# Weight sums in place, two blocks per split, first rows on VectorE, and a mixed order of pairs in a transformer-block kernel

## The chip, the core and the metric

The kernel runs on one core of a Trainium2 chip. The metric is the device time of one execution in microseconds (us); lower is better. In the rows the engines are PE (TensorE, matmuls; PEld its weight loads), DVE (VectorE), ACT (ScalarE), POOL (GpSimd) and SP (SyncE, which here issues DMAs only).

## The reference

One layer over 1024 positions of width 1024, all in float32:

- u = rmsnorm(x); z = u @ w_in gives a_b, a_c, a_x (512 each), q_lat (384), kv_lat (256), k_rope (32), gate_a, gate_b (1024 each)
- a gated causal width-3 depthwise convolution of these, and latent attention (8 heads, low-rank keys and values, rotary part, block-causal mask); h = x + rmsnorm((sigmoid(gate_a) * ya + sigmoid(gate_b) * yb) @ w_o)
- up = conv3(rmsnorm(h) @ w_ffn_up) + b, width 2 x 2816; f = (gelu(up_gate) * up_val) @ w_ffn_down; h = h + rmsnorm(f)
- out = h + rmsnorm((p @ w_ple_proj) * sigmoid(h @ w_ple_gate))

## The kernel before, in words

Everything is kept transposed: 128 features on the partitions, 1024 positions along the row, cut into two halves of 512. On-chip memory is dealt by hand as 51 numbered slots of 1024 float32 per partition (`f32(i)`, `single(i, h)` for a half); eight groups of four adjacent slots (`QUADS`) can be read by one instruction over four halves.

A float32 operand is used as two rounded parts: `split` makes `hi` by a ScalarE cast (L174) and `lo = src - hi` by a subtraction on VectorE or GpSimd (L175). A product of 128 x 512 outputs then takes three passes (hi hi, lo hi, hi lo). `block` splits one 512-wide half of a weight tile into one slot of the ring `wblk` (hi in the slot's first half, lo in its second); the ring has seven slots.

The three large matrix products (w_in, w_ffn_up, the first 16 of 22 row blocks of w_ffn_down) are done by a Winograd form of Strassen's scheme, seven block products for eight. The right operand's seven combinations (B11, B21, B22, T2, T4, T3, T1) come from `x_blocks` in three stages, all on VectorE but for the casts: `first` (B11, B21), `second` (B22, T2 and four 128x2048 subtractions, L268), `third` (T3, T4, T1). `second` needs the second half of the positions, `first` only the first half. The left side comes as pairs of weight tiles: `pair` loads two tiles, forms S1 to S4 (L325 to L327, L363), and runs seven products of 12 matmuls each (`prod`, L289). `first_row` runs two of the seven ahead (A11 B11 and A12 B21), while the right operand's other combinations are still being made; the pair that follows runs the other five (`early`). S1 stands in a half slot of its own (ring `s1s`), and the T1 product is copied out by ScalarE (L358) into another (`m5s`) and added by GpSimd (L359).

Stages: the norm of x and the p projection (to about 43 us), six first rows and the pairs of the gates, convolution mixer and latents (to 370), projections and attention (to 630), w_o and a norm, twelve first rows of the up projection (to 830), its 22 pairs (to 1200: first the twelve with a first row, of which eight had been stored to DRAM in `d_z` and are loaded again, then ten without), down in two groups of four first rows and four pairs and a plain tail (to 1437), then the second norm and the last gate. After each up pair the two results go through the convolution (ScalarE L517, four VectorE steps L519, in PSUM), the gelu (L897) and a product (L898), and the tile goes to DRAM (`d_f`); down loads these tiles again into four-slot groups (`u0`, `u1` in `plans`), and the lists in `plans` say which slots hold which combination. In down's second group the results are added to the first group's (`add`).

A scheduler writes each engine's instruction order: it takes what is ready by its own estimate of times, earlier program text first. On the chip each engine keeps that order; a waiting instruction holds all behind it.

Of the kernel before, what the change touches and what calls it, by code (L numbers as in the profile page):

```python
# [57 lines left out]
class Ring:  # L58
# [6 lines left out]
    def __call__(self):  # L65
        self.n += 1
        return self.items[(self.n - 1) % len(self.items)]


@with_exitstack  # L70
def kernel(
# [170 lines left out]

    who = dict(S1=G, S3=G, bS1=V, bS3=G, bS4=G, fw=G)

    def x_blocks(u, slots):

        names = ("B11", "B21", "B22", "T2", "T4", "T3", "T1")
        where = {n: slots[4 * i : 4 * i + 4] for i, n in enumerate(names)}
        B = {}
# [16 lines left out]
        def sub(dst, a, b):  # L266
            d, a_, b_ = (several(u[k : k + 4], F32, h) for k, h in (dst, a, b))
            V.tensor_sub(d, a_, b_)  # L268

        def second():  # L270
# [6 lines left out]
            sub(b21, b21, b22)  # L277
# [243 lines left out]
    for g in range(2):  # L521
        ys = [34, 35]
        v, e = f32(47), f32(48)
        for j in range(2):
            ct = 2 * g + j
            pair(w_in[4 + ct], w_in[8 + ct], B, raws, s1s, m5s, mm, v, e)
# [4 lines left out]
        pair(w_in[2 * g], w_in[2 * g + 1], B, raws, s1s, m5s, mm, v, e)  # L531
# [24 lines left out]
    m5s = Ring(singles(50))  # L556
# [18 lines left out]
    raws = Ring([7, 8])  # L575
    lraw = Ring([46, 45, 47])
# [255 lines left out]
    u = list(range(34, 42))  # L832
# [283 lines left out]
```

## Time and profile before

| | |
|---|---|
| time, median of 3 runs | 1557.64 us (1552.98 to 1557.90) |
| profiled execution, its own time | 1554.84 us |
| its span, first to last instruction | 1553.0 us |
| mean granted TensorE clock | 0.986 of full |
| DMA moved | 195.59 MB, 126 GB/s |

Idle time of an engine matters only where TensorE waits for it.

### The profile page before, as it was taken

The numbers are of one execution on the slowest core, as the hardware profiler recorded it, in microseconds if no ns is written. First come the engines' busy times: TensorE is split into PE (matmuls) and PEld (weight loads), VectorE is DVE, ScalarE is ACT, GpSimd is POOL, SyncE is SP. The second block draws the span as 40 slices with busy tenths as digits, with TensorE's granted clock in tenths as the row PEclk, the third lists the DMA queues.
The fourth block names the chain that finished last, engine by engine and source line by source line (L and its number), as shares of the span: only waits on it lengthen the run. The fifth ranks groups of instructions, "written<-read, shape, count | busy, mean of one in ns | idle before, by whom it ended". The sixth has DMA issues, their size and how long they took to land. (4 is left out here: it accounts for less than half of the span.)

```text
span 1553.0 us, 19627 instructions
## 1 busy us (share of the span) xinstructions
PE 1483.4 (96%) x6980; PEld 1228.1 (79%) x6980; DVE 1161.7 (75%) x1645; ACT 726.4 (47%) x1266; POOL 759.9 (49%) x561
## 2 busy tenths in 40 slices
PE   8999999999989999999998999999999897999997
PEld 6778888887768888888886876788887785788786
DVE  6996666656478887925688899888878879648776
ACT  8534323445357777334444544444445343234533
POOL 3744454427344334434355434444434465687853
PEclk9999999999999999999999999999999999999998
DMA  9334222326831013624362433322224533253322
GB/s 335 128 125 179 86 91 68 122 96 230 267 116 52 28 56 110 205 78 149 106 236 67 161 141 117 108 88 90 91 85 163 176 95 117 87 164 108 127 91 96
DMA packets 72642, 195.59 MB, mean 126 GB/s; under 512 B 7264, under 2 KB 22112, under 8 KB 72544
## 3 DMA queue, kind: packets, MB, share of 16 engines
q1 hardware_dynamic: 64192, 169.89, 33.0%
q10 hardware_dynamic: 8352, 24.44, 4.1%
q8 instruction: 55, 0.90, 0.2%
q14 instruction: 43, 0.35, 0.1%
HBM read 142.79 MB, written 51.51 MB: 125 GB/s over the span
## 5 line engine op out<-in xcount | busy, mean ns | idle before, releaser
L289 PE MATMUL psum<-s,s 128*128 128x512 f32 x3948 | 921.2, 394 | 33.0 <-DVE s L175 8.1
L289 PEld LDWEIGHTS psum<-s,s 128*128 128x128 f32 x3948 | 744.8, 190 | 203.7 <-DVE s L175 12.6
L175 POOL TENSOR_TENSOR s<-s,s 128x512 fp32r<-128x512 f32 (+1 forms) x298 | 441.2, 1492 | 379.2 <-ACT s L174 363.5
L174 ACT CAST s<-s 128x512 fp32r<-128x512 f32 (+2 forms) x572 | 357.8, 657 | 452.8 <-PE psum L289 128.4
L202 PE MATMUL psum<-s,s 128*128 128x512 f32 (+1 forms) x1920 | 412.4, 373 | 12.3 <-ACT s L174 10.5
L202 PEld LDWEIGHTS psum<-s,s 128*128 128x128 f32 x1920 | 335.7, 191 | 73.3 <-ACT s L174 13.3
L175 DVE TENSOR_TENSOR s<-s,s 128x512 fp32r<-128x512 f32 (+2 forms) x274 | 280.6, 1037 | 48.7 <-ACT s L174 45.5
L519 DVE SCALAR_TENSOR_TENSOR psum<-s,vecs,psum 128x1023 f32<-128x1023 f32 (+1 forms) x88 | 111.5, 1281 | 19.3 <-ACT psum L517 17.9
L237 DVE TENSOR_TENSOR s<-s,s 128x512 f32<-128x512 f32 (+1 forms) x83 | 74.9, 903 | 56.9 <-ACT s L234 54.6
L326 POOL TENSOR_TENSOR s<-s,s 128x512 f32<-128x512 f32 x47 | 68.5, 1458 | 96.3 <-DMA s<-in_w_up_dram 42.9
L325 POOL TENSOR_TENSOR s<-s 128x512 f32<-128x512 f32 x47 | 65.0, 1384 | 93.8 <-DMA s<-in_w_up_dram 32.7
L359 POOL TENSOR_TENSOR s<-s,s 128x512 f32<-128x512 f32 x43 | 57.8, 1344 | 92.0 <-ACT s L358 91.8
L175 DVE TENSOR_TENSOR s<-psum,s 128x512 fp32r<-128x512 f32 (+3 forms) x144 | 70.9, 505 | 31.3 <-ACT s L174 30.2
L174 ACT CAST s<-psum 128x512 fp32r<-128x512 f32 (+3 forms) x144 | 61.1, 444 | 36.0 <-PE psum L774 9.8
L750 POOL TENSOR_SCALAR s<-s,ri 128x384 f32<-128x384 f32 (+5 forms) x48 | 41.3, 861 | 70.3 <-DVE ri L749 55.5
L363 DVE TENSOR_TENSOR s<-s 128x512 f32<-128x512 f32 x47 | 49.5, 1054 | 30.9 <-POOL s L175 30.6
L234 ACT ACTIVATE s<-s 128x512 f32<-128x512 f32 (+1 forms) x82 | 47.8, 590 | 52.8 <-DVE s L1004 23.9
L737 PE MATMUL psum<-s,s 128*128 128x512 f32 (+2 forms) x288 | 67.4, 359 | 2.3 <-ACT s L748 2.2
L327 DVE TENSOR_TENSOR s<-s,s 128x512 f32<-128x512 f32 x47 | 44.6, 948 | 22.4 <-POOL s L326 22.0
L517 ACT ACTIVATE psum<-s,vecs 128x1024 f32<-128x1024 f32 x44 | 52.8, 1207 | 17.4 <-POOL s L359 11.4
L762 PE MATMUL psum<-s,s 128*128 128x256 f32 x320 | 54.1, 292 | 1.5 <-DVE s L175 0.7
L748 ACT ACTIVATE s<-psum,nm 128x128 f32<-128x128 f32 (+3 forms) x64 | 47.5, 745 | 14.2 <-DVE nm L746 9.0
(116 smaller groups left out, 1122.9 us busy)
## 6 DMA issues: line engine op xcount, KB each, us to landing
s<-in_w_up_dram SPq DMA_DIRECT2D x56, 512.0 KB, 3.7
s<-in_w_in_dram SPq DMA_DIRECT2D x40, 512.0 KB, 3.7
s<-in_w_down_dram SPq DMA_DIRECT2D x36, 512.0 KB, 3.6
d_f<-s SPq DMA_DIRECT2D x22, 512.0 KB, 2.7
s<-d_f SPq DMA_DIRECT2D x22, 512.0 KB, 5.4
s<-in_x_dram SPq DMA_DIRECT2D x32, 256.0 KB, 5.4
d_sg<-s ACTq DMA_DIRECT2D x16, 512.0 KB, 2.9
s<-d_sg SPq DMA_DIRECT2D x16, 512.0 KB, 3.9
```

Of the source, the lines that this page charges most:

```text
L174: A.copy(hi, src)
L175: (eng or V).tensor_sub(lo, src, f(hi))
L202: nc.tensor.matmul(out_ps, w[c // HALF][pw][:, c % HALF : c % HALF + P], X[k][half][px][:, cs], start=start and a == 0 and k == 0, stop=st ...
L237: V.tensor_add(acc, acc, sq)
L289: nc.tensor.matmul(pt, w[pw][:, k * P : (k + 1) * P], blk[k][px], start=a == 0 and k == 0, stop=a == 2 and k == 3,)
L325: who["S1"].tensor_add(s1, a21, a22)
L326: who["S3"].tensor_sub(a21, a11, a21)
L359: G.tensor_add(d22, d22, m5)
L517: A.activation(dst, src, AF.Identity, bias=bias, scale=w2)
L519: V.scalar_tensor_tensor(dst[:, i:], src[:, : S - i], w, dst[:, i:], op0=ALU.mult, op1=ALU.add)
L737: nc.tensor.matmul(st_[:, lo_ : lo_ + w_], q[part_q][:, o : o + P], parts(K[hd, kh])[part_k][:, 0:w_], start=part_q == 0 and part_k == 0, ...
L762: nc.tensor.matmul(po[:, 0:256], vt[:, kt, :], t_[:, kk * 256 : (kk + 1) * 256], start=kt == 0 and part == 0, stop=kt == 2 * b + 1 and par ...
```

## The change

- `pair`: S1 overwrites a22 (after a22 is split for the T4 product), S3 overwrites a21, S2 overwrites a11, and S4 overwrites a12. The rings `s1s` and `m5s` are gone. `wide` splits a whole weight tile at once: hi of both blocks in one slot, lo in another. A11/A12, S2/S4 and S3/S1 are split so; A22 alone by `block`. The order of products becomes A11, A12, S2, S3, S1, A22, S4. The T1 product is added twice by VectorE. `who` names the engines of A11/A12's split, A22's split and the two sums.
- `first_row`: the weights' split is one `wide` on VectorE.
- `x_blocks`: the order of stage three is T3, T1, T4, and its VectorE instructions are queued behind the last subtraction of stage two.
- The slots freed join `wblk`: nine slots in the gate and up stages.
- Up: the twelve pairs with a first row stand between the ten without (0 without, 1 with, 2 without, ...); the convolution of a pair comes after the next pair in the program; the last tile's comes inside down's first group.
- Down: another dealing of slots; each group's first pair has its splits and sums on VectorE; the plain tail's six tiles come by halves through one slot.

```diff
+    def become(self, items):
+
+        k = self.n % len(self.items)
+        old = self.items[k:] + self.items[:k]
+        self.items = [i for i in items if i not in old] + [i for i in old if i in items]
+        self.n = 0
...
+    def wide(src, eng):
+        hi, lo = f32r(wblk()), f32r(wblk())
+        split(src, hi, lo, eng)
+        return [(hi[:, hs(i)], lo[:, hs(i)]) for i in range(2)]
...
-        names = ("B11", "B21", "B22", "T2", "T4", "T3", "T1")
+        names = ("B11", "B21", "B22", "T2", "T3", "T1", "T4")
...
         def third():
-            operand("T3", 0, 1)
-            operand("T4", 4, 0)
-            operand("T1", 0, 0)
+            with tc.issue_after(t4[0].ins):
+                operand("T3", 0, 1)
+                operand("T1", 0, 0)
+                operand("T4", 4, 0)
...
-        w = load_w(src, raws, eng=who["fw"])
+        raw = f32(raws())
+        nc.sync.dma_start(raw, src)
+        w = wide(raw, V)
...
+    def pair(src0, src1, B, raws, banks, out0, out1, early=False, hooks=(), add=None, who=(V, G, G, G)):
...
         if not early:
-            A11 = block(a11, V)
-        s1 = single(*s1s())
-        who["S1"].tensor_add(s1, a21, a22)
-        who["S3"].tensor_sub(a21, a11, a21)
-        V.tensor_sub(a11, s1, a11)
-        S2 = block(a11, V)
-        S3 = block(a21, who["bS3"])
+            A11, A12 = wide(r0, who[0])
+        A22 = block(a22, who[1])
+        who[2].tensor_add(a22, a21, a22)
+        who[3].tensor_sub(a21, a11, a21)
+        V.tensor_sub(a11, a22, a11)
+        V.tensor_sub(a12, a12, a11)
+        S2, S4 = wide(r0, V)
+        S3, S1 = wide(r1, V)
+        m1, u3 = (d12, d21) if add is None else add
+        u2 = m1
         if not early:
             A.copy(m1, times(A11, "B11"))
+            V.tensor_add(d11, times(A12, "B21"), m1)
         V.tensor_add(u2, times(S2, "T2"), m1)
         V.tensor_add(u3, times(S3, "T3"), u2)
-        A22 = block(a22, V)
-        pt = times(A22, "T4")
...
+        pt = times(S1, "T1")
...
+        V.tensor_add(d22, u3 if add is None else d22, pt)
         V.tensor_add(d12, d12, pt)
...
-            m5 = single(*m5s())
-            A.copy(m5, pt)
-            G.tensor_add(d22, d22, m5)
-        if not early:
-            A12 = block(a12, G)
-            V.tensor_add(d11, d11, times(A12, "B21"))
-        V.tensor_sub(a12, a12, a11)
-        S4 = block(a12, who["bS4"])
+        V.tensor_add(d21, d21, times(A22, "T4"))
         pt = times(S4, "B22")
...
+    wblk.become([*range(NBLK), 33, 50])
...
+    wblk.become([*range(NBLK), 45, 50])
...
+    rows = [1, 3, 5, 7, 8, 10, 11, 13, 14, 16, 18, 20]
+    early = dict(zip(rows[:4], (44, 33, 46, 47)))
+    spilled = rows[4:]
...
+        pair(w_up[j], w_up[NFF + j], B, raws, mm, f32(z0), f32(z1), j in early or j in spilled, who=(G, G, G, G))
...
+    last = up(0)
+    for j in range(1, NFF):
+        now = up(j)
+        gated(*last)
+        last = now
...
     plans = (
-        (range(9, 13), range(21, 25), [29, 25, 38, 13, 0, 17, 21]),
-        (range(9, 13), range(29, 33), [13, 17, 0, 21, 38, 25, 29]),
+        (range(9, 13), range(13, 17), [21, 25, 29, 38, 17, 0, 9]),
+        (range(13, 17), range(21, 25), [25, 38, 17, 0, 9, 29, 13]),
     )
+    u3s = singles(24)
...
+        raws = Ring([7, 8] if g else [7, 8, 45])
...
         second()
+        if g == 0:
+            free = [50]
+            gated(*last)
         third()
...
+                add=(m1s[i], single(*u3s[i % 2])) if g else None, who=(V, G, G, G) if i else (V, V, V, V),
             )
+            mm = Ring(range(6))
...
+    fops = [[*range(25, 29), 38, 39], [*range(29, 33), 17, 18]]
+    fraw = Ring(singles(21))
```

## Rows read from the trace of the kernel before

**Rows 1.** Busy time of each engine over the span: us, share, instructions.

```profile
PE 1483.4 (96%) x6980; PEld 1228.1 (79%) x6980; DVE 1161.7 (75%) x1645; ACT 726.4 (47%) x1266; POOL 759.9 (49%) x561
```

**Rows 2.** Windows: stretch, length, busy us (instructions) of PE, PEld, DVE, ACT, POOL, PEclk, DMA.

```profile
43.00:100.00 57.00, 53.45 (x225) 43.38 (x224) 56.06 (x59) 27.33 (x40) 33.51 (x18) 0.94 0.29 95
100.00:370.00 270.00, 270.00 (x1216) 224.14 (x1215) 176.01 (x255) 110.31 (x186) 129.74 (x95) 1.00 0.36 124
800.00:842.00 42.00, 35.30 (x136) 26.09 (x135) 39.24 (x34) 17.78 (x24) 19.35 (x12) 0.92 0.22 67
...
875.00:1000.00 125.00, 119.12 (x509) 94.06 (x508) 117.21 (x124) 55.74 (x76) 55.02 (x41) 1.00 0.37 126
1000.00:1173.00 173.00, 173.00 (x765) 143.26 (x764) 133.76 (x161) 79.67 (x113) 69.83 (x54) 1.00 0.26 86
1173.00:1225.00 52.00, 46.31 (x190) 37.15 (x189) 50.16 (x42) 28.06 (x38) 24.09 (x14) 0.93 0.41 146
...
1275.00:1330.00 55.00, 45.71 (x180) 34.95 (x179) 50.23 (x42) 20.78 (x32) 33.18 (x21) 0.94 0.31 105
1330.00:1371.00 41.00, 39.11 (x170) 31.37 (x169) 27.34 (x32) 13.93 (x25) 31.91 (x23) 1.00 0.37 107
```

**Rows 3.** Windows inside two of the switches between matrix products.

```profile
801.00:834.00 33.00, 26.30 (x105) 18.89 (x103) 33.00 (x27) 15.31 (x22) 14.19 (x8) 0.97 0.17 48
...
1185.00:1213.00 28.00, 22.31 (x94) 17.60 (x93) 27.96 (x19) 15.49 (x20) 14.64 (x9) 0.96 0.37 130
```

**Rows 4.** Groups by line and form: shapes, count, busy us, mean ns, idle before.

```profile
L175 POOL TENSOR_TENSOR s<-s,s 128x512 fp32r<-128x512 f32 x290 | 433.3, 1505 | 360.7 <-ACT s L174 345.0 <-PE psum L202 10.3 <-PE psum L762 1.8
...
L175 DVE TENSOR_TENSOR s<-s,s 128x512 fp32r<-128x512 f32 x217 | 196.6, 911 | 41.3 <-ACT s L174 38.2 <-PE psum L289 1.3
L175 DVE TENSOR_TENSOR s<-s,s 128x1024 fp32r<-128x1024 f32 x52 | 79.8, 1566 | 4.2 <-ACT s L174 4.2
...
L325 POOL TENSOR_TENSOR s<-s 128x512 f32<-128x512 f32 x47 | 65.0, 1384 | 93.8 <-DMA s<-in_w_up_dram 32.7 <-DMA s<-in_w_down_dram 18.1 <-DVE s L175 13.5
...
L174 ACT CAST s<-s 128x1024 fp32r<-128x1024 f32 x52 | 52.8, 1049 | 47.5 <-DVE s L268 31.4 <-DVE s L175 9.4 <-DVE s L858 3.0
...
L338 DVE TENSOR_TENSOR s<-psum,s 128x512 f32<-128x512 f32 x47 | 32.2, 685 | 17.9 <-PE psum L289 9.8 <-issue 4.7 <-ACT s L337 3.4
...
L898 DVE TENSOR_TENSOR s<-s,psum 128x1024 f32<-128x1024 f32 x22 | 26.7, 1214 | 2.3 <-ACT s L897 2.3
...
L268 DVE TENSOR_TENSOR s<-s,s 128x2048 f32<-128x2048 f32 x8 | 20.9, 2616 | 0.0
```

**Rows 5.** DVE in order of time in one up pair: start us, us, instruction.

```profile
957.27 0.68 DVE L339 TENSOR_TENSOR s<-psum,s 128x512 f32<-128x512 f32 x1
957.87 1.27 DVE L519 SCALAR_TENSOR_TENSOR psum<-s,vecs,psum 128x1022 f32<-128x1022 f32 x1
959.05 1.23 DVE L175 TENSOR_TENSOR s<-s,s 128x512 fp32r<-128x512 f32 x1
...
964.86 1.77 DVE L327 TENSOR_TENSOR s<-s,s 128x512 f32<-128x512 f32 x1 [0.71 <-POOL s L326]
```

**Rows 6.** PE in order of time: runs of matmuls, idle before and releaser.

```profile
954.42 3.04 PE L289 MATMUL psum<-s,s 128*128 128x512 f32 x12 [0.82 <-DVE s L338]
...
970.18 1.19 PE L289 MATMUL psum<-s,s 128*128 128x512 f32 x4 [0.74 <-DVE s L338]
...
1211.76 28.62 PE L289 MATMUL psum<-s,s 128*128 128x512 f32 x113 [4.69 <-DVE s L306]
...
1292.24 15.83 PE L289 MATMUL psum<-s,s 128*128 128x512 f32 x60 [3.30 <-ACT s L358]
1310.59 4.17 PE L289 MATMUL psum<-s,s 128*128 128x512 f32 x16 [2.51 <-ACT s L174]
...
1320.16 20.82 PE L289 MATMUL psum<-s,s 128*128 128x512 f32 x84 [1.52 <-DVE s L175]
```

**Rows 7.** POOL in order of time at down's second group.

```profile
1307.71 2.17 POOL L325 TENSOR_TENSOR s<-s 128x512 f32<-128x512 f32 x1 [4.64 <-DVE s L175]
```

More of the change, by code (lines that the diff above doesn't have):

```diff
@@ L525 @@
             ct = 2 * g + j
-            pair(w_in[4 + ct], w_in[8 + ct], B, raws, s1s, m5s, mm, v, e)
+            pair(w_in[4 + ct], w_in[8 + ct], B, raws, mm, v, e)
             V.tensor_mul(v, v, e)
@@ L575 @@
     raws = Ring([7, 8])
+    wblk.become(range(NBLK))
     lraw = Ring([46, 45, 47])
@@ L829 @@
             split(ya_, *mX[ft][h])
-    u = list(range(34, 42))
+    u = [*range(38, 42), *range(34, 38)]
     wos = load_all(w_o, raws, range(25, 34))
@@ L862 @@
             second()
-    s1s = Ring(singles(50))
-    m5s = Ring([(45, 1)])
-    zs, ts_ = Ring([34, 35, 36, 37]), Ring([48, 49])
+    wblk.become([*range(NBLK), 45, 50])
+    free = [48, 49, 34, 35, 36, 37]
     tps = Ring([4, 6])
-    early = [44, 33, 46, 47]
-    spilled = 8
-    NE = len(early) + spilled
-    for j in range(NE):
-        z0 = f32(early[(j - NE) % len(early)])
+    rows = [1, 3, 5, 7, 8, 10, 11, 13, 14, 16, 18, 20]
+    early = dict(zip(rows[:4], (44, 33, 46, 47)))
+    spilled = rows[4:]
+    for n, j in enumerate([*spilled, *early]):
+        z0 = f32([*early.values()][n % 4])
         first_row(w_up[j], B, raws, mm, z0[:, hs(0)], z0[:, hs(1)])
-        if j < spilled:
+        if j in spilled:
             nc.sync.dma_start(d_z[j], z0)
@@ L880, with up, gated @@
     mm = Ring(range(4))
-    for n, j in enumerate([*range(spilled, NE), *range(spilled), *range(NE, NFF)]):
-        if n:
-            late = [z0, z1]
-        z0 = early[n] if n < len(early) else zs()
-        z1 = zs()
-        if n < len(early):
-            zs.items.append(z0)
-        if len(early) <= n < NE:
+    def up(j):
+        z0 = early[j] if j in early else free.pop(0)
+        if j in spilled:
             nc.sync.dma_start(f32(z0), d_z[j])
-        pair(w_up[j], w_up[NFF + j], B, raws, s1s, m5s, mm, f32(z0), f32(z1), n < NE)
+        z1 = free.pop(0)
+        pair(w_up[j], w_up[NFF + j], B, raws, mm, f32(z0), f32(z1), j in early or j in spilled, who=(G, G, G, G))
+        return j, z0, z1
+    def gated(j, z0, z1):
         cv = []
@@ L895 @@
             cv.append(t)
-        fo = f32(ts_())
-        A.activation(fo, cv[0], AF.Gelu_apprx_tanh)
-        V.tensor_mul(fo, fo, cv[1])
-        nc.sync.dma_start(d_f[j], fo)
-    mm = Ring(range(6))
-    raws = Ring([7, 8])
-    late = [z0, z1, *late]
-    rest = [i for i in zs.items if i not in late]
-    yacc = [i for two in zip(rest, late) for i in two]
-    extra = [42, 43, 48, 49]
+        fo = free.pop(0)
+        A.activation(f32(fo), cv[0], AF.Gelu_apprx_tanh)
+        V.tensor_mul(f32(fo), f32(fo), cv[1])
+        nc.sync.dma_start(d_f[j], f32(fo))
+        free.extend([z0, z1, fo])
+    last = up(0)
[3 more added lines that the diff above has]
+        last = now
+    raws = Ring([7, 8])
+    wblk.become(range(NBLK))
+    extra = [i for i in free if i not in quad_of][-2:]
+    free = [i for i in free if i not in extra]
+    yacc = [i for two in zip(free[:4], [*free[4:], *last[1:]]) for i in two]
+    extra = [42, 43, *extra]
+    m1s = [single(*i) for i in singles(45, 50)]
     plans = (
-        (range(9, 13), range(21, 25), [29, 25, 38, 13, 0, 17, 21]),
-        (range(9, 13), range(29, 33), [13, 17, 0, 21, 38, 25, 29]),
+        (range(9, 13), range(13, 17), [21, 25, 29, 38, 17, 0, 9]),
+        (range(13, 17), range(21, 25), [25, 38, 17, 0, 9, 29, 13]),
     )
+    u3s = singles(24)
     for g, (u0, u1, starts) in enumerate(plans):
@@ L956, in down @@
         V.tensor_add(y, y, pt)
-    fs = [(c, f_tiles(ks)) for c, ks in ((16, range(16, 20)), (20, range(20, 22)))]
-    hrs = Ring(singles(38, 39))
-    sqs, sqs2, accs = Ring(singles(48)), Ring(singles(49)), Ring(singles(50))
+    fs = ((16, fX[:4]), (20, fX[4:]))
+    hrs = Ring(singles(24, 21))
+    sqs, sqs2, accs = Ring(singles(extra[2])), Ring(singles(extra[3])), Ring(singles(50))
     hX = [[None, None] for _ in range(8)]
+    hslots = range(9, 17), [*range(17, 21), *range(38, 42)]
     SS, RB = 6, 7
@@ L985 @@
                 for o in range(c_ * n, (c_ + 1) * n):
-                    down(fX, w, h, o)
+                    down(fX_, w, h, o)
         second_residual(h)
```

81 lines of the change are left out of this document (25 added, 56 removed).

## The prediction

> **What bounds the kernel now.** I read the busy times first, then the windows, then each window's waits. The reader sees TensorE at 96% of the span and VectorE, next, at 75% [rows 1], so an edit counts only where TensorE starts late. The windows give its pace: from 1000 to 1173 us it starts 765 matmuls and never stops, 173.0/764 = 226.4 ns each; 100 to 370 is as dense [rows 2]. The change leaves the number of matmuls alone (2 products per first row, 5 per pair behind one, 7 per whole pair, 12 matmuls each), so it can give back only lost time: a window's length less its starts times 226.4 ns [rows 2]:
>
> - A, 43 to 100 (switch to the gates' pairs): 57.0 - 225 x 0.2264 = 6.1 us
> - B, 800 to 842 (switch to the up projection): 42.0 - 30.8 = 11.2
> - C, 875 to 1000 (up pairs behind a first row): 125.0 - 115.2 = 9.8
> - D, 1173 to 1225 (up to down): 52.0 - 43.0 = 9.0
> - E, 1275 to 1330 and 1330 to 1371 (down's first to second group): 14.2 + 2.5 = 16.7
>
> That is 52.8 us of the execution's 1554.84 (span 1553.0, 1.84 around it). At the switches VectorE has no gap: 33.00 of 33 us at B, 27.96 of 28 at D [rows 3]. TensorE's stops there end on it, directly (4.69 at 1211.76, 1.52 at 1320.16) or through ScalarE behind it (3.30 at 1292.24) [rows 6]. In C one pair takes 970.18 - 954.42 = 15.76 us [rows 6] where 60 matmuls take 13.6: VectorE's work for a pair is longer than TensorE's.
>
> **Prices.** VectorE reading PSUM: the next instruction 0.60 us later, a convolution step 1.18 later [rows 5]; 128x1024 from PSUM 1.21, near 1.13 as a step [rows 4]. With both sources in SBUF a 128x512 one is as short when GpSimd rests, but 1.77 beside it [rows 5]; over the run 0.91 at 512 wide, 1.57 at 1024, 2.62 at 2048 [rows 4]. PSUM-sourced ones stay at 0.68 [rows 4]. So GpSimd's work slows exactly the splits and sums. GpSimd takes 1.50 for a split, 1.38 for a sum [rows 4].
>
> **The change part by part.**
>
> *Pairs (47).* The weight sums go into the loaded tiles, two blocks are split by one 1024-wide cast and subtraction, and the copy of the T1 product with its GpSimd addition becomes a second VectorE addition from PSUM. On VectorE a pair behind a first row had 5 SBUF steps and 5 PSUM steps; it gets 2 sums, 2 wide splits and 6 PSUM steps: 2 x 0.60 + 2 x 1.13 + 6 x 0.60 = 7.1 clean against 6.0. On GpSimd it has one split and two sums, 4.25, for two splits and three sums, 7.1. Per pair VectorE works 1.1 more and waits less.
>
> *C, the mixing of the up projection.* With convolution (4 x 1.18) and product (1.13) a short pair costs VectorE 7.1 + 5.85 = 12.95 clean. Before it was 6.0 + 5.85 = 11.85 in a cycle of 15.76 that was almost all VectorE, so about 3 to 4 us were contention; GpSimd's share of it falls by 4.25/7.1, so I take 1.8: 14.75 (bounds 12.95, no contention, and 16.9, all of it). A whole pair adds one PSUM step, 13.55, and, as GpSimd there also splits A11 and A12 (a 128x1024 subtraction, not in this trace: between 1.50 and 2 x 1.50; I take 2.8, nearer the second, since the length doubles), about 2.5 contention: 16.0. TensorE has 13.6 and 19.0. Before, the twelve short ones ran in a row, each 2.2 late, and the slack of the ten whole ones came after; now at most two short ones stand together, 2.3 us behind, and the whole pair next to them has 3.0 to spare. In sum VectorE needs 12 x 14.75 + 10 x 16.0 = 337 of TensorE's 12 x 13.6 + 10 x 19.0 = 353. So C's 9.8 go to about 2: gain 7.5, bounds -6 (16.9 per short pair: 12 x 3.3 less 10 x 2.4) and 9.8.
>
> A rule weighed here: a VectorE instruction with two SBUF sources took 1.77 instead of 0.68 beside GpSimd [rows 5]. The Trainium skill (SBUF — State Buffer, section Who interferes with whom) calls it an exclusive lock held for a whole instruction, the later one blocked fully. It speaks against the wide GpSimd split: by it a VectorE sum could wait 2.8 where 1.5 was the most, 10 x 1.3 = 13 us more on VectorE in the up stage; by the row's 1.1 of waiting, nothing more. By the rule the sum stays, as the whole pairs have 10 x 3.0 to spare.
>
> *First rows.* Their weights' splits go from GpSimd (2 x 1.50) to one VectorE subtraction (1.13 to 1.57), at A six, at B twelve (about six of them after VectorE is full), at D and E four each: 6.8 to 9.4 more on VectorE at A and B, 4.5 to 6.3 at D and E. This is put on the engine that has no gap. What pays for it: some ten 1024-wide splits and four 2048-wide subtractions at a switch lose contention, 10 x 0.36 (1.57 - 1.21) + 4 x 0.3 = 4.8, of which I count 3, as the pairs' GpSimd work stays. Net +4 on VectorE at A and B, +2 at D and E.
>
> *Order.* The splits of T3, T1 and T4 may no longer slip ahead of the last subtraction, and the T4 product is moved behind T1. This brings T2 forward and gives T4 another product's time, 2.7. At A that is all there is against +4: gain 0, bounds -5 and 4. At B the first up pair is now a whole one: A11 and A12 need B11 and B21 alone, 24 x 0.2264 = 5.4 us of TensorE work before T2 is wanted. The 8% half clock in this window, 0.92 [rows 2], costs 42 x 0.08 = 3.4 and goes if no stop is long. 11.2 + 4 - 5.4 - 2.7 - 3.4 = 3.7 left: gain 7.5, bounds 1 and 11.
>
> *D.* VectorE: first rows +2, the first pair entirely on VectorE 5.4 clean for 3.0, so +2.4; the last tile's convolution and product, 5.85, moved behind T2's preparation, so -5.85 ahead of it and +5.85 ahead of T3 and the first pair's splits. Ahead of T2 about 1.5 less, behind it no less than before. The first rows keep 4 PSUM banks instead of 6, so a late addition stops TensorE sooner. Of 9.0 I take back 2; bounds -8 (convolution and sums, 5.85 + 2.4, late in full) and 9.
>
> *E.* Here GpSimd's first sum starts at 1307.71, having waited 4.64 for VectorE [rows 7]: it writes slot 9, which holds an operand still to be split. ScalarE's casts stand behind it: TensorE stops 2.51 before 1310.59, and from there to 1320.16 three runs of 16, 4 and 4 matmuls, 5.4 us of work, take 9.6 [rows 6]. In-place sums need no such slot, so these 6.7 us should go. B11's operands get slots that are free after the first rows, so 2.3 of splits and one 2.2 subtraction leave the full stretch: +2 + 2.4 - 4.5 = 0 for VectorE before T2, but the chain starts sooner. Of 16.7 I keep 5.5: gain 11, bounds 4 (the slot alone, less 3) and 16.7.
>
> *Slots held longer.* A wide pair of slots is free only after both its products. With nine slots (gates, up) the tightest reuse leaves two products, 5.4 us; in down, with seven, S2/S4 and S3/S1 of the next pair wait for a product that ends one product ahead, 2.7 us. Needed: cast 1.05 [rows 4], subtraction 1.57, less 0.9, as the first four matmuls use the cast alone: 1.7. What is queued ahead on ScalarE (0.6) and VectorE (0.6 to 1.2) decides. 12 such places: 0 to 12 x 1.2 = 14; I take 4.
>
> *Nothing elsewhere.* From 100 to 370 VectorE is busy 176 of 270 us [rows 2], and 17 pairs x 1 us more is hidden in the rest; without it 17 x 1 would show (bounds 0 and 17, I take 0). The down tail's tiles pass through two half slots, during the second group and 144 matmuls (32.6 us) of its first half.
>
> Sum: 0 + 7.5 + 7.5 + 2 + 11 - 4 = 24. 1554.84 - 24 = 1530.8. The runs' median, 1557.64, lies 2.8 above the profiled execution, so I say 1533.
>
> **Rivals.**
>
> 1. *VectorE stays full at the switches.* For: no gap there now [rows 3], and 7 to 9 us are added at each. Against: contention falls. Then A -3, B +4, C +7.5, D -5, E +9, slots -4: gain 8.5, 1549.
> 2. *Slots, the slower side.* In the up stage a reused wide slot has 5.4 us. Cast 1.05, split 1.57, less 0.9, plus one convolution instruction on ScalarE (1.2) and two steps on VectorE (2.4) queued ahead make 5.3: at the edge. If contention (1.1 per split) tips it, each of 22 pairs loses up to 1.5, and down's 12 places 1.2 each: 33 + 10 more than counted, 1576. It decides from 1.1 us per up pair (24/22). For: today each block has its own slot and the whole pairs lose nothing at 1000 to 1173. Against: VectorE has gaps in whole pairs (133.8 of 173 busy [rows 2]).
> 3. *The losses go nearly whole*, 45 of 52.8: 1512. For: the causes are few and named. Against: the work is still VectorE's.
>
> That the mixing doesn't do what it says is the lower end of C: 7.5 + 6 less, 1546.
>
> **How the numbers follow.** Forecast 0.60 (own range 1519 to 1548), rival 1 0.17, rival 2 0.14, rival 3 0.09. From 1514 to 1560 leaves out most of rival 2, half of rival 3 and small tails, 0.2. About 0.3% (1553 to 1562) is what a measurement of this kernel can tell from no change. Faster: 0.58 + 0.11 + 0.09 = 0.78; same: 0.02 + 0.05 + 0.03 = 0.10; slower 0.12.
>
> **What would show it.** In the up stage: no regular stop in any pair, VectorE near 90%, GpSimd near 30%; a stop at each pair's second product speaks for rival 2. At the start of up: TensorE with A11 and A12 while VectorE subtracts. At D: VectorE full and TensorE stopping on T3 speaks for rival 1. In the second down group the first pair's sums must start before T1's split; if TensorE still stops some 2 us there, E is wrong. The stretch 100 to 370 should stay dense. The forecast is wrong if C still loses over 6 or the switches together over 25.

## The result, and the profile after

The changed kernel takes 1546.08 us (median of 5 runs, 1545.17 to 1547.52), a ratio of 0.993 to before (95% interval 0.9913 to 0.9948). That is 11.6 us faster. The forecast was 24.6 us: the sign was right, the time lies in the range, and the gain is under half of what was forecast. The profiled execution took 1545.98 us, its span 1544.1.

The page's busy times, beside [rows 1]: VectorE has 13 us more, GpSimd 215 less.

```profile
PE 1476.6 (96%) x6980; PEld 1225.9 (79%) x6980; DVE 1174.8 (76%) x1663; ACT 689.0 (45%) x1082; POOL 545.0 (35%) x402
```

The windows of [rows 2], same columns. They are cut at the same times, not at the same work: counted in matmuls, the changed kernel is 2 to 3 us behind the one before from 150 to 800, some 9 ahead from 1000 to 1225, 1 ahead at 1250 and 4 ahead at 1330.

```profile
43.00:100.00 57.00, 54.17 (x231) 42.13 (x230) 52.78 (x59) 28.37 (x36) 19.39 (x9) 1.00 0.28 95
100.00:370.00 270.00, 267.71 (x1202) 221.21 (x1201) 179.01 (x251) 97.19 (x129) 70.00 (x55) 1.00 0.36 120
800.00:842.00 42.00, 36.65 (x156) 28.04 (x155) 38.60 (x38) 18.26 (x22) 20.25 (x10) 0.98 0.18 60
875.00:1000.00 125.00, 125.00 (x553) 103.58 (x552) 110.34 (x122) 51.76 (x53) 39.13 (x27) 1.00 0.35 114
1000.00:1173.00 173.00, 173.00 (x765) 143.36 (x764) 155.66 (x170) 74.99 (x77) 52.57 (x35) 1.00 0.35 118
1173.00:1225.00 52.00, 44.87 (x189) 36.36 (x187) 49.31 (x48) 25.67 (x30) 0.57 (x1) 0.93 0.63 219
1275.00:1330.00 55.00, 46.13 (x192) 36.61 (x192) 47.75 (x41) 20.60 (x29) 30.33 (x19) 0.94 0.41 124
```

C (875 to 1000) has 553 matmuls for 509 and no gap; D has one fewer, with GpSimd at rest; the loss at 43 to 100 goes on behind 100. To compare kernels I sum, over a stretch, by how much the distance of two matmul starts exceeds the usual one: 227 ns for 512 columns (the pace of the dense stretches), for narrower matmuls the usual distance of their own width. The stretches are wide enough to hold nearly the same work in every kernel: A 25 to 150, B 800 to 850, C 850 to 1000, D 1175 to 1250, E 1250 to 1375, tail from 1375.

| lost us | A | B | C | D | E | tail | all |
|---|---|---|---|---|---|---|---|
| before | 6.9 | 11.7 | 9.6 | 9.1 | 17.2 | 14.0 | 101.1 |
| changed | 9.1 | 10.3 | 0.0 | 17.1 | 12.7 | 10.5 | 92.6 |
| gain | -2.3 | 1.4 | 9.6 | -8.0 | 4.5 | 3.5 | 8.5 |
| forecast | 0 | 7.5 | 7.5 | 2 | 11 | 0 | 24, with -4 for slots |

The 8.5 are nearly all of the span's 8.9 (1553.0 less 1544.1). So C came in full, D went the other way, B and E came short.

TensorE in order of time in the changed kernel, at its long stops (as [rows 6]; idle before and releaser in brackets):

```profile
839.50 0.73 PE L300 MATMUL psum<-s,s 128*128 128x512 f32 x2 [1.82 <-DVE s L182]
841.72 8.52 PE L300 MATMUL psum<-s,s 128*128 128x512 f32 x24 [1.49 <-DVE s L182]
...
1211.42 13.13 PE L300 MATMUL psum<-s,s 128*128 128x512 f32 x48 [6.67 <-DVE s L319]
1229.76 7.33 PE L300 MATMUL psum<-s,s 128*128 128x512 f32 x24 [5.22 <-DVE s L349]
...
1321.57 8.65 PE L300 MATMUL psum<-s,s 128*128 128x512 f32 x30 [6.44 <-DVE s L350]
```

B still loses to VectorE's splits (L182): T2's second and T4's first. D has two stops, of 6.67 on a first row's addition (L319) and 5.22 on the first pair's (L349); E has one of 6.44 on the first pair's L350. All three are additions that read PSUM. What VectorE does ahead of them in D:

```profile
1199.03 2.30 DVE L278 TENSOR_TENSOR s<-s 128x2048 f32<-128x2048 f32 x1
1201.23 7.04 DVE L182 TENSOR_TENSOR s<-s,s 128x1024 fp32r<-128x1024 f32 x8
...
1209.97 1.30 DVE L319 TENSOR_TENSOR s<-psum,s 128x512 f32<-128x512 f32 x2
...
1218.58 2.36 DVE L182 TENSOR_TENSOR s<-s,s 128x1024 fp32r<-128x1024 f32 x2 [0.97 <-ACT s L181]
1222.28 1.23 DVE L182 TENSOR_TENSOR s<-s,s 128x1024 fp32r<-128x1024 f32 x1 [1.34 <-ACT s L181]
1223.54 2.29 DVE L278 TENSOR_TENSOR s<-s 128x2048 f32<-128x2048 f32 x1
1225.87 3.23 DVE L278 TENSOR_TENSOR s<-s,s 128x2048 f32<-128x2048 f32 x1
1229.03 0.68 DVE L349 TENSOR_TENSOR s<-psum,s 128x512 f32<-128x512 f32 x1
```

Eight splits stand ahead of L319: two of T3, four halves of T1, two of T2 (all splits have the line L182, and the row counts both widths as one form; which operand one belongs to is told by its place in VectorE's instruction list, here and below). From 1218.58 on three splits and two 2048-wide subtractions (L278) stand ahead of L349. The second of the three splits is the first pair's own, of S2 and S4; the other two (of B11) and the subtractions are preparation of the second group. Its inputs now have slots of their own, so it came forward from E into D.

L319 is not all of the stop of 6.67. What TensorE takes up first behind it is T4, which is written into the slots of T1's source, so ScalarE's casts for T4 wait for T1's splits:

```profile
1206.10 1.99 ACT L181 CAST s<-s 128x1024 fp32r<-128x1024 f32 x2 [3.45 <-DVE s L182]
```

The first of these two casts ends at 1207.14, so I estimate that at most 1211.42 - 1207.14, some 4 us of the 6.67, hang on the place of L319.

### The profile page after: what moved, and what is told of

Same layout as the page of the kernel before. It is cut to its first block, busy times and chain, and to the rows that moved or that the text cites. A ratio compares the mean times of both kernels' runs of the same rounds, so it can differ in the third digit from the quotient of the medians.

```text
span 1544.1 us, 19277 instructions
## 1 busy us (share of the span) xinstructions
PE 1476.6 (96%) x6980; PEld 1225.9 (79%) x6980; DVE 1174.8 (76%) x1663; ACT 689.0 (45%) x1082; POOL 545.0 (35%) x402
## 5 line engine op out<-in xcount | busy, mean ns | idle before, releaser
L300 PEld LDWEIGHTS psum<-s,s 128*128 128x128 f32 x3948 | 743.1, 189 | 199.6 <-DVE s L182 16.9
L181 ACT CAST s<-s 128x512 fp32r<-128x512 f32 (+3 forms) x431 | 340.1, 811 | 477.0 <-PE psum L300 157.6
L182 POOL TENSOR_TENSOR s<-s,s 128x512 fp32r<-128x512 f32 (+2 forms) x186 | 280.4, 1520 | 726.2 <-PE psum L300 423.7
L215 PEld LDWEIGHTS psum<-s,s 128*128 128x128 f32 x1920 | 335.6, 191 | 77.5 <-ACT s L181 15.5
L182 DVE TENSOR_TENSOR s<-s,s 128x1024 fp32r<-128x1024 f32 (+2 forms) x245 | 308.7, 1278 | 46.6 <-ACT s L181 44.2
L513 DVE SCALAR_TENSOR_TENSOR psum<-s,vecs,psum 128x1023 f32<-128x1023 f32 (+1 forms) x88 | 111.7, 1280 | 1.0
L250 DVE TENSOR_TENSOR s<-s,s 128x512 f32<-128x512 f32 (+1 forms) x83 | 65.9, 797 | 42.6 <-ACT s L247 40.6
L182 DVE TENSOR_TENSOR s<-psum,s 128x512 fp32r<-128x512 f32 (+3 forms) x144 | 70.8, 504 | 27.5 <-ACT s L181 26.3
L339 POOL TENSOR_TENSOR s<-s,s 128x512 f32<-128x512 f32 x43 | 65.0, 1513 | 3.3
L357 DVE TENSOR_TENSOR s<-s,psum 128x512 f32<-128x512 f32 x47 | 32.1, 683 | 34.0 <-PE psum L300 31.4
L731 PEld LDWEIGHTS psum<-s,s 128*128 128x128 f32 x288 | 46.4, 189 | 9.9 <-ACT s L742 5.3
L742 ACT ACTIVATE s<-psum,nm 128x128 f32<-128x128 f32 (+3 forms) x64 | 47.5, 745 | 14.3 <-DVE nm L740 8.9
L756 PEld LDWEIGHTS psum<-s,s 128*128 128x128 f32 x320 | 45.5, 189 | 6.0 <-DVE s L182 2.0
```

Source lines behind the costliest of these rows:

```text
L181: A.copy(hi, src)
L182: (eng or V).tensor_sub(lo, src, f(hi))
L215: nc.tensor.matmul(out_ps, w[c // HALF][pw][:, c % HALF : c % HALF + P], X[k][half][px][:, cs], start=start and a == 0 and k == 0, stop=st ...
L250: V.tensor_add(acc, acc, sq)
L300: nc.tensor.matmul(pt, w[pw][:, k * P : (k + 1) * P], blk[k][px], start=a == 0 and k == 0, stop=a == 2 and k == 3,)
L339: who[3].tensor_sub(a21, a11, a21)
```

## The experiments

Two theories. **Order**: VectorE's queue is fixed beforehand, and additions that free PSUM stand in it behind preparation. **Load**: VectorE has simply too much to do at the switches. Each kernel is the changed one with the edit shown, 5 rounds beside the kernel before. What they lost (us, as above):

| kernel | ratio, 95% | A | B | C | D | E |
|---|---|---|---|---|---|---|
| unmixed | 0.9953, 0.994 to 0.9967 | 9.1 | 12.3 | 0.0 | 17.8 | 12.9 |
| gfirst | 0.9874, 0.986 to 0.9889 | 5.2 | 8.5 | 0.0 | 14.2 | 11.2 |
| vhalf | 0.9933, 0.9921 to 0.9945 | 7.8 | 11.1 | 0.0 | 17.7 | 13.0 |
| hold2 | 0.9941, 0.9927 to 0.9955 | 12.3 | 10.4 | 0.0 | 17.4 | 12.6 |
| six | 0.9925, 0.9912 to 0.9937 | 9.5 | 10.3 | 0.0 | 16.4 | 12.7 |
| vggg | 0.9959, 0.9946 to 0.9973 | 9.9 | 9.5 | 0.0 | 18.7 | 12.9 |
| nodefer | 0.9924, 0.9911 to 0.9937 | 9.9 | 10.6 | 0.7 | 14.2 | 13.1 |
| t2first | 0.9949, 0.9937 to 0.9962 | 11.1 | 6.6 | 0.0 | 18.4 | 14.3 |
| tail | 0.9958, 0.9944 to 0.9972 | 9.4 | 11.0 | 0.0 | 17.2 | 12.6 |
| evac | 0.9989, 0.9976 to 1.0003 | 8.9 | 10.4 | 0.0 | 18.7 | 17.0 |
| gbest | 0.9884, 0.9871 to 0.9898 | 5.2 | 9.5 | 0.0 | 16.5 | 9.1 |
| best2 | 0.9905, 0.989 to 0.992 | 5.2 | 9.5 | 0.0 | 18.8 | 10.1 |
| best3 | 0.9864, 0.9848 to 0.988 | 3.5 | 7.2 | 0.0 | 15.8 | 9.6 |
| firsthold | 0.9882, 0.9865 to 0.99 | 5.2 | 8.6 | 0.0 | 16.6 | 8.1 |
| firstholdnodefer | 0.9857, 0.984 to 0.9873 | 5.2 | 9.3 | 0.0 | 12.3 | 8.5 |
| allorder | 0.9914, 0.9899 to 0.9929 | 4.5 | 7.2 | 0.0 | 14.0 | 19.9 |
| best4 | 0.9849, 0.9824 to 0.9874 | 4.5 | 7.2 | 0.0 | 14.2 | 9.0 |
| best5 | 0.9837, 0.9816 to 0.9858 | 4.5 | 7.2 | 0.0 | 12.7 | 10.9 |

A stretch that an edit doesn't touch moves by up to 1 (A by 3 once, hold2): no verdict rests on less.

**Mixing (unmixed).**

```diff
-    rows = [1, 3, 5, 7, 8, 10, 11, 13, 14, 16, 18, 20]
+    rows = [8, 9, 10, 11, *range(8)]
-    last = up(0)
-    for j in range(1, NFF):
+    last = up(8)
+    for j in [*rows[1:], *range(12, NFF)]:
```

> The changed kernel with the up projection's order of before: twelve short pairs in a row, then the ten whole ones; all else as changed. Mixing theory: the 9.6 us that the stretch 875 to 1000 got back are lost again, since a short pair costs VectorE more than TensorE's 13.6 us, and the first pair no longer has its A11 and A12 products in front of T2: 1546 + 9.6 + 1 to 4 = 1556 to 1560, with a regular stop in each short pair. Rival (the pairs' new form, with less GpSimd work beside VectorE, would have done it alone): no regular stops, 1546 to 1549.

1548.57 us. The theory that C needs the mixing fell: twelve short pairs in a row lose nothing. The window of C, and VectorE in one short pair of this kernel:

```profile
875.00:1000.00 125.00, 125.00 (x553) 103.49 (x552) 121.80 (x137) 57.83 (x59) 45.68 (x28) 1.00 0.43 143
```

```profile
930.64 0.68 DVE L340 TENSOR_TENSOR s<-s,s 128x512 f32<-128x512 f32 x1
...
932.43 0.68 DVE L350 TENSOR_TENSOR s<-psum,s 128x512 f32<-128x512 f32 x1
933.03 0.68 DVE L341 TENSOR_TENSOR s<-s 128x512 f32<-128x512 f32 x1
...
946.03 0.68 DVE L350 TENSOR_TENSOR s<-psum,s 128x512 f32<-128x512 f32 x1
```

GpSimd beside it:

```profile
939.02 1.29 POOL L182 TENSOR_TENSOR s<-s,s 128x512 fp32r<-128x512 f32 x1 [8.69 <-PE psum L300]
```

From L350 to L350 it is 13.60 us, TensorE's own 60 x 0.2267. The in-place sums (L340, L341) take 0.68 where the sum before took 1.77 [rows 5]: they need GpSimd's two sums, now its last work for the pair, which ends at 930.3, and GpSimd rests for 8.69 us behind it. From 875 to 975 VectorE's instructions with two SBUF sources took 3.1 us beyond their uncontended times (0.68, 1.22 at 1024 wide); before it was 16.5. That is 0.4 a pair for 2.6. What mixing does is B's 2.0 (12.3 to 10.3); as a time, the two intervals overlap, so the kernels are not told apart.

**First rows (gfirst, vhalf).**

```diff
-        w = wide(raw, V)
+        w = [block(raw[:, hs(c)], G) for c in range(2)]   # vhalf: V for G
```

> The changed kernel with the first rows' weights split on GpSimd again, as two 512-wide subtractions. Rival theory (VectorE is simply full at the switches, 26 splits of 1.1 to 1.6 us too many): the stops of the switches shrink, D from 17 to about 11 us lost and E from 13 to 9, B by 2: about 1534. Order theory (the stops come from evacuations of PSUM that are queued behind preparation): VectorE has less work but the same order, contention comes back, the stops near 1204, 1224 and 1315 us stay within 2 us each: 1544 to 1549.

> The changed kernel with the first rows' weights still split on VectorE, but as two 512-wide subtractions in slots of their own, as where GpSimd did them (1536). It parts that gain: if it came from taking the work off VectorE, this one has the same work there (2 x 0.60 for 1.13 us a row) and stays at 1544 to 1549. Rival (the halves and their slots did it, since a product can start after the first half): 1536 to 1540.

1536.06 and 1545.28 us. Half the width alone does nothing that the intervals tell; taking the splits off VectorE as well gives 9.2 us more (10.0 against the changed kernel), spread over all four switches (A 3.9, B 1.8, D 2.9, E 1.5). So far load. But D keeps its stops: in gfirst, VectorE ahead of the L319 that ends one of 4.43 at 1200.97,

```profile
1189.89 2.28 DVE L278 TENSOR_TENSOR s<-s 128x2048 f32<-128x2048 f32 x1
1192.10 4.76 DVE L182 TENSOR_TENSOR s<-s,s 128x1024 fp32r<-128x1024 f32 x6
1196.78 1.27 DVE L513 SCALAR_TENSOR_TENSOR psum<-s,vecs,psum 128x1022 f32<-128x1022 f32 x1
1197.96 2.35 DVE L182 TENSOR_TENSOR s<-s,s 128x1024 fp32r<-128x1024 f32 x2
1200.23 0.68 DVE L319 TENSOR_TENSOR s<-psum,s 128x512 f32<-128x512 f32 x1
```

does 10.3 us of other work, nearly all preparation: a subtraction, splits of T3, T1 and T2, and one convolution step (L513).

**One wait of D at a time (hold2, six, vggg, nodefer).**

```diff
 # hold2 (done holds each pair's last addition)
-        first()
+        with tc.issue_after(done[0][1].ins) if g else ExitStack():
+            first()
 # six: before down; Ring(range(4)) again after gated(*last)
+    mm = Ring(range(6))
 # vggg
-who=(V, G, G, G) if i else (V, V, V, V),
+who=(V, G, G, G),
 # nodefer: behind the up loop, not in down
+    gated(*last)
```

> The changed kernel with the VectorE part of the second down group's B11 and B21 preparation queued behind the first group's first pair's last addition. Order theory: the first pair's evacuation no longer stands behind four splits and two 2048-wide subtractions, the stop near 1224 us (5.4, and about 1 of half clock after it) goes to under 1: 1539 to 1541, and 1275 to 1375 loses no more than before. Rival (VectorE full): the same work is only late elsewhere, the second group's T2 comes later by about as much: 1545 to 1547.

> The changed kernel with six PSUM banks instead of four for the first group's first rows in down; the first pair gets four, the later ones six, as changed. Order theory: TensorE can run two more products while the first-row additions wait behind VectorE's preparation, so the stop near 1204 us (6.8) goes to under 3 and the half clock after it with it: 1540 to 1543. Rival (VectorE full): the stop only moves to the first pair's T2 or T3, 1545 to 1547.

> The changed kernel with down's first pairs as the others: A22's split and the two sums on GpSimd instead of VectorE. Load theory: 3 x 0.6 us and their contention leave VectorE at D and again at E, each loses 1.5 to 3 us less: 1540 to 1543. Rival (GpSimd's chain of 1.50 and 2 x 1.38 us stands ahead of the first pair's S2 and makes it late): D and E lose 2 to 4 us more each, 1549 to 1554.

> The changed kernel with the last up tile's convolution and product traced before down's first rows, as before the change. Load theory: 5.85 us of VectorE's work come ahead of T2 instead of behind it, D loses 3 to 6 us more: 1549 to 1552. Rival (in the changed kernel most of the convolution stands ahead of the first rows' additions anyway, so that the deferral is no deferral): 1544 to 1547.

1546.62, 1543.32, 1549.25 and 1544.11 us: hold2 and six shortened the stop that they were made for, nodefer took 2.9 from D, and none of these three is told from the changed kernel by its interval. Vggg is some 3 to 4 us slower, at the edge of what the intervals tell; its time is in its rival's range, but D and E lose only 1.6 and 0.2 more, where the rival said 2 to 4 each. Hold2 shows where the time goes. TensorE, then ScalarE:

```profile
1228.47 4.01 PE L300 MATMUL psum<-s,s 128*128 128x512 f32 x16 [0.79 <-DVE s L349]
1233.21 2.12 PE L300 MATMUL psum<-s,s 128*128 128x512 f32 x8 [0.73 <-POOL s L182]
1237.67 2.12 PE L300 MATMUL psum<-s,s 128*128 128x512 f32 x8 [2.34 <-ACT s L181]
1241.69 6.67 PE L300 MATMUL psum<-s,s 128*128 128x512 f32 x21 [1.89 <-DVE s L182]
```

```profile
1227.22 0.62 ACT L181 CAST s<-s 128x512 fp32r<-128x512 f32 x1 [1.47 <-DMA s<-in_w_down_dram]
1230.60 0.62 ACT L181 CAST s<-s 128x512 fp32r<-128x512 f32 x1 [2.75 <-DMA s<-in_w_down_dram]
```

The wait for L349 is down from 5.22 to 0.79, but the pairs behind the first now stop TensorE three times. Weights of the third pair land only at 1227, and half of the second's at 1230 (releaser DMA). That half goes into slot 50, which holds the last up tile's product until that is stored. On SP's queue the second group's eight loads stand first, then this store (1218.38), then the third pair's loads (1220.11, 1223.70), and the load into slot 50, which has to wait for the store to land, comes only at 1225.89.

**Load and late weights together (firsthold, firstholdnodefer).** The edits are gfirst with hold2, and these with nodefer, which frees slot 50.

> The changed kernel with the first rows' weights on GpSimd in halves and the second group's B11 and B21 preparation held behind the first group's first pair. Load theory: both together take some 13 us of work from VectorE between the first subtraction and the first pair's last addition, about what the change put there; D comes to 8 to 11, 1530 to 1532. Rival (the weights of the second pair are late, since the last up tile's product takes their slot 50 and the loads stand behind it on SP's queue): D stays at 13 to 16, 1534 to 1537.

> The last kernel with the last up tile's convolution before down, so that slot 50 is free for the second pair's weights. If the slot made the second pair late: D 8 to 10, 1529 to 1532. If what is left is the order on VectorE (convolution and splits ahead of the first rows' additions): D 13 to 16 as in the kernels without the hold, 1534 to 1538.

1536.09 and 1532.41 us. VectorE's work from the first 2048-wide subtraction of D to the first pair's last addition, split into its uncontended steps and the rest:

| kernel | uncontended | contention | D lost |
|---|---|---|---|
| before | 42.3 | 9.2 | 9.1 |
| changed | 56.0 | 2.8 | 17.1 |
| gfirst | 50.5 | 3.5 | 14.2 |
| hold2 | 48.2 | 2.1 | 17.4 |
| firsthold | 44.3 | 3.3 | 16.6 |

With the work of before (44.3 for 42.3), less contention and 10.5 us of idle time on VectorE, D still loses 16.6. Load alone falls there. In firstholdnodefer, without the shared slot, the later stop of 2.44 is gone and D loses 12.3, between the two ranges stated for it. Nodefer also moves the convolution, so the slot's part of this is not held apart. TensorE in firsthold, then in firstholdnodefer:

```profile
1201.13 5.49 PE L300 MATMUL psum<-s,s 128*128 128x512 f32 x12 [4.41 <-DVE s L319]
1222.39 7.59 PE L300 MATMUL psum<-s,s 128*128 128x512 f32 x32 [0.79 <-DVE s L349]
1232.41 17.80 PE L300 MATMUL psum<-s,s 128*128 128x512 f32 x70 [2.44 <-ACT s L181]
```

```profile
1201.66 4.95 PE L300 MATMUL psum<-s,s 128*128 128x512 f32 x12 [6.42 <-DVE s L319]
1208.11 30.91 PE L300 MATMUL psum<-s,s 128*128 128x512 f32 x132 [1.50 <-ACT s L181]
```

From 1208.11 it runs 30.91 us without a stop. Left is the stop of 6.42 on a first row's addition behind preparation.

**Order at B and E (t2first, tail, evac).**

```diff
 # t2first: operand() returns its last subtraction
-            operand("T2", 4, 1)
-            t4.append(sub(b21, b21, b22))
+            with tc.issue_after(operand("T2", 4, 1).ins):
+                t4.append(sub(b21, b21, b22))
 # tail (done[2][0]: the third pair's second GpSimd sum)
+            with tc.issue_after(done[2][0].ins):
                 split(raw, *fX[k][h], V if h else G)
 # evac (behind: the T3 addition of the pair before, in down)
+        with tc.issue_after(behind.ins) if behind else ExitStack():
             V.tensor_sub(a11, a22, a11)
             V.tensor_sub(a12, a12, a11)
```

> The changed kernel with the last 2048-wide subtraction queued on VectorE behind T2's splits, at all four switches. If the order on VectorE matters at B: T2, the operand wanted first after A11 and A12, is there 2.3 to 3.4 us sooner, B loses 3 us less (10.3 to 7), A, D and E 0 to 1 each: 1541 to 1543. If only the load matters: T3's splits are as late as before, the stop moves from T2 to T3 and the time stays, 1545 to 1547.

> The changed kernel with GpSimd's splits of the last six tiles queued behind the second group's third pair's sums (until then they stand between the sums of its first pairs). If GpSimd's queue makes E late: pair 1's sums come some 4 us sooner, the stop of 6.6 near 1315 us goes to under 2 with its half clock: 1539 to 1542. If VectorE's load does: the stop stays over 5, 1545 to 1547. A loss of its own is possible after the second group, if the tiles come late: up to 3 us.

> The changed kernel with, in down, each pair's two VectorE sums (and so the splits that need them) queued behind the second PSUM addition (T3's) of the pair before it. Order theory for E: the first pair's two additions no longer stand behind the second pair's chain (sums, cast and split, 1313.3 to 1320.1 us); that chain takes some 4 us and then has three more products, 8 us, of cover; the stop of 6.6 near 1315 us goes to under 2, E from 12.7 to 7 or 8, and D keeps its 17: 1540 to 1542. Rival (the second pair's chain is then late by as much and TensorE stops at its S2): E 11 to 14, 1545 to 1549.

1547.11, 1548.37 and 1553.61 us. T2first took 3.7 from B, as expected of order, and lost 2.0 at A, 1.3 at D and 1.6 at E. A moves by as much in kernels that don't touch it; for D and E the subtraction and T3, which now come later, are a likely reason that I did not follow up. Tail left E as it was: GpSimd's tile splits were not the cause. Evac removed the stop of 6.44, and lost more; a stop of about 1 us straddles 1250 there, so its D and E can each be read 1 higher or lower. Its VectorE in E (the sums are L341 and L342 there, the T2 and T3 additions L350 and L351):

```profile
1318.65 0.69 DVE L350 TENSOR_TENSOR s<-psum,s 128x512 f32<-128x512 f32 x1 [7.01 <-PE psum L300]
...
1319.98 0.72 DVE L341 TENSOR_TENSOR s<-s 128x512 f32<-128x512 f32 x1
...
1322.33 4.55 DVE L182 TENSOR_TENSOR s<-s,s 128x1024 fp32r<-128x1024 f32 x2
...
1334.11 0.69 DVE L350 TENSOR_TENSOR s<-psum,s 128x512 f32<-128x512 f32 x1 [4.75 <-PE psum L300]
```

VectorE waits 7.01 and 4.75 for TensorE, so it isn't full here; a pair's two sums and two wide splits take 1319.98 to 1326.8, 6.8 us against 3.5 clean, as GpSimd works beside the splits. Put ahead of all additions of the pair before, this chain stops TensorE there (6.44 in the changed kernel); put behind them all, it is late for its own pair. The rival's range (E 11 to 14) was too small, at 17.0.

There is an order between the two, and firsthold, which loses 8.1 at E, has it. Its VectorE there (sums L340 and L341, the T2 and T3 additions L349 and L350):

```profile
1308.96 1.67 DVE L341 TENSOR_TENSOR s<-s 128x512 f32<-128x512 f32 x1
1310.55 0.68 DVE L349 TENSOR_TENSOR s<-psum,s 128x512 f32<-128x512 f32 x1
...
1311.94 2.16 DVE L182 TENSOR_TENSOR s<-s,s 128x1024 fp32r<-128x1024 f32 x1
```

The second pair's sums stand ahead of the first pair's additions, its split behind them, and TensorE stops for 0.99 in place of 6.44. VectorE also has less to do there than in the changed kernel, so this is not yet the order alone.

**Towards a better kernel (gbest, best2, best3, allorder, best4, best5).** Edits: gbest is gfirst, vggg and six; best2 gfirst, nodefer and six banks for all of down; best3 that with t2first and tail; allorder is best2 with hold2, t2first and T2's part queued behind the second first row's addition; best4 firstholdnodefer with t2first; best5 that with each group's second pair entirely on VectorE as well.

> The changed kernel with three edits: the first rows' weights on GpSimd in halves, down's first pairs with GpSimd's split and sums, six PSUM banks for down's first rows. Load theory: 1536 less 2 to 6 for the first pairs and the banks: 1530 to 1534. Rival (GpSimd becomes the late one at D and E, with 8 more splits and 3 more instructions of a pair in the same stretch): 1537 to 1541.

> The changed kernel with the first rows' weights on GpSimd in halves (1536), the last up tile's convolution before down and six PSUM banks for all of down. Load theory: alone, the undone deferral took D from 17.1 to 14.2 and the first rows to 14.2; both take away VectorE work or a wait at one place, together D comes to 8 to 11, near the 9.1 of before: 1530 to 1533. Rival (they shorten the same stop): D 13 to 15, 1535 to 1537.

> The last kernel with T2's splits ahead of the last subtraction, and the last tiles' GpSimd splits behind the third pair's sums, as well. Order at B and GpSimd's queue at E as causes: 1531 less 3 and less 5, 1523 to 1527. If load alone decides: as the last kernel, 1529 to 1533.

> The last kernel with T2's splits ahead of the last subtraction, with six PSUM banks for all of down, and in down with T2's splits, the last subtraction and what follows it queued behind the second first row's addition. Order as the cause of the rest: D 6 to 9, B 7, A 3.5, 1524 to 1528. Rival (T2 now comes late for the first pair, and TensorE stops there instead): D 13 or more, 1530 to 1534.

> The best kernel so far (first rows' weights on GpSimd, last up tile before down, second group's preparation held; 1532) with T2's splits ahead of the last subtraction. T2 came sooner in the two kernels with this order (B 7.2 against 9.5 without it, A 3.5 against 5.2): 1528 to 1530 if D and E keep their 12.3 and 8.5; if the queue of D is dealt worse by it, as where this order was put into the changed kernel alone (D 18.4 against 17.1), 1531 to 1534.

> The same, with the second pair of each down group entirely on VectorE too, which has idle time there now. If GpSimd's chain (split and two sums, 4 us and more) makes the second pair late, D and E lose 1 to 2 us less each: 1526 to 1529. Rival (VectorE's queue there is what counts): 1 to 3 us more, 1530 to 1534.

1537.61, 1539.99, 1532.95, 1541.16, 1532.33 and 1530.78 us. The gains of single edits do not add: best2 joins two that each had D at 14.2 and has 18.8, with one stop of 10.93. Allorder put two of the first rows' additions of D ahead of the preparation; the other two still stand behind the splits of T3 and T1, and a stop of 5.38 at 1209.16 ends on the last of them. So all additions ahead of the preparation is not tried; D is 14.0, and E loses 19.9. In time best2 and allorder lie above all that was stated for them, the other four in their rival's range. Best5 is the fastest, 0.9837 of before; by the intervals it beats the changed kernel and is not told from best3, best4 or firstholdnodefer.

## Why the gain was under half of the forecast

- **A, gain 0: -2.3**, inside its bounds. First rows on VectorE were booked at +4 there, and gfirst gives 3.9 back. That an earlier T2 would pay for them is not seen, for T2 does not come earlier (see B).
- **B, gain 7.5: 1.4. Two terms failed.** "A11 and A12 [...] 5.4 us of TensorE work before T2 is wanted": this cover is worth 2.0 (unmixed). And "This brings T2 forward" came out the other way round. VectorE at B, in the kernel before and in the changed one:

```profile
817.04 2.35 DVE L175 TENSOR_TENSOR s<-s,s 128x1024 fp32r<-128x1024 f32 x2
...
821.00 3.37 DVE L268 TENSOR_TENSOR s<-s 128x2048 f32<-128x2048 f32 x1
824.29 4.52 DVE L175 TENSOR_TENSOR s<-s,s 128x1024 fp32r<-128x1024 f32 x2
```

```profile
824.79 3.37 DVE L278 TENSOR_TENSOR s<-s 128x2048 f32<-128x2048 f32 x1
828.09 5.71 DVE L182 TENSOR_TENSOR s<-s,s 128x1024 fp32r<-128x1024 f32 x4
...
834.32 1.21 DVE L182 TENSOR_TENSOR s<-s,s 128x1024 fp32r<-128x1024 f32 x1
...
837.16 5.65 DVE L182 TENSOR_TENSOR s<-s,s 128x1024 fp32r<-128x1024 f32 x3
```

  Before, the two splits at 817.04 are T3's, and T2's come right behind the last subtraction, at 824.29. In the changed kernel the four at 828.09 are T3's and T1's, held behind the subtraction, and T2's come behind those, at 834.32 and first at 837.16: 9.5 us from the subtraction's start for 3.3 before. At A, D and E, too, T3's and T1's splits now stand between the last subtraction and T2's. With T2 ahead of subtraction, T3 and T1 (t2first) B loses 6.6, nearer the 3.7 forecast. The half clock, -3.4, did not go either: it ran for some 6.8 us in both kernels (granted clock 0.50 from 831.8 to 838.6 before and from 840.2 to 847.0 in the changed one, there mostly behind the window's end).
- **C, gain 7.5: 9.6, for another reason.** The contention of a short pair was taken as 1.8, scaled by GpSimd's work; it is 0.4, since the sums form a chain with GpSimd's. At 121.80/125 of 13.6, 13.3, VectorE fits a short pair without mixing.
- **D, gain 2: -8.0. The step that failed worst.** E's "2.3 of splits and one 2.2 subtraction leave the full stretch" was booked as a gain in E only; where they would go was not asked. They went to D, with more: "behind it no less than before" became 13.7 us more uncontended VectorE work ahead of the first pair's last addition, of which hold2 takes 7.8 and gfirst 5.5 away. The deferral was priced on VectorE alone; its slot 50 and SP's queue were not followed, though the second pair's weights wait there. The remark that four banks stop TensorE sooner got no price, and "gives T4 another product's time" is void where T4 waits for T1's source, as here. Gfirst, hold2 and nodefer together bring D from 17.1 to 12.3; the other 3.2 above the 9.1 of before stay open.
- **E, gain 11: 4.5. Mis-sized.** The slot's stop went, as forecast, and B11's preparation too; but the in-place chain, "2 x 0.60 + 2 x 1.13" = 3.5, takes 6.8 beside GpSimd (evac, whole). In the changed kernel its two sums and first split stand ahead of the first pair's additions, from 1313.3 to 1320.1, and TensorE stops for 6.44.
- **Slots, -4: 0.** From 1000 to 1173 nothing is lost, nor at a pair's second product elsewhere in up; in down TensorE runs 55.64 us from 1238.84, through the first group's later pairs, without a stop. Rival 2 is refuted.
- **Tail, 0: 3.5 gained**, not forecast. The kernel before has stops of 2.02 (at 1450.11) and 3.23 (at 1495.16) ahead of a norm's one-column matmuls, and the changed one has neither; why is not tested.

Rival 1 (VectorE stays full at the switches, 1549) came closest in time and in nearly every stretch; its mechanism is half of it, for at D the loss stayed where VectorE had idle time. About the rule weighed there (the Trainium skill, SBUF — State Buffer, section Who interferes with whom): the wide GpSimd split takes 2.41 us, and in the up projection all ten of them lay beside VectorE instructions that read PSUM, so no run here shows what it does to a sum with two SBUF sources.

Open: why D still loses some 3 us more than before even in firstholdnodefer and best5; what all first rows' additions ahead of the preparation would do there; and how much of firsthold's E is its order and how much its lighter VectorE.

## What to carry to other kernels

When work leaves a full stretch, ask where it goes: new slots let it start early, in the stretch before, on the same engine. At a switch, read the queue and not only the load: an addition that frees PSUM behind 10 us of preparation stops TensorE as surely as a full engine, and an edit that mends one stretch can deal the queues anew in another, so don't count on the gains of single edits to add. When you hold work back, ask what it now stands in front of: T3 held behind a subtraction came to stand ahead of T2. Follow each deferred result to its slot and to the load that waits for that slot.

## What was not expected of the hardware

GpSimd's subtraction of 128x1024 takes less than two halves (1.49 each). In the short pairs of C shown, VectorE's two 512-wide sums don't contend (0.68), as a chain puts them behind GpSimd's last work. GpSimd's groups by form in the changed kernel:

```profile
L182 POOL TENSOR_TENSOR s<-s,s 128x512 fp32r<-128x512 f32 x168 | 248.3, 1491 | 679.2 <-PE psum L300 423.7 <-ACT s L181 253.1 <-PE psum L756 1.8
L182 POOL TENSOR_TENSOR s<-s,s 128x1024 fp32r<-128x1024 f32 x10 | 24.1, 2409 | 26.5 <-ACT s L181 26.5
```

The estimate in the prediction was 2.8; 2.41 is measured. At B the granted clock of 800 to 842 rose from 0.92 [rows 2] to 0.98, and fell right behind it: after two stops of 1.82 and 1.49, 24 matmuls from 841.72 took 8.52 us, where the dense pace makes 5.4.
